# Output projection to up projection: weight sums of the first two units moved ahead, and the last row block put in a manual order

## The chip, the cores and the metric

The kernel runs on one core of a Trainium2 chip. The metric is the device time of one execution in microseconds (us). The kernel before was timed three times: 1768.19, 1768.23 and 1777.83 us, median 1768.23. Engines are named as in the profile: PE is TensorE (matmuls), ACT is ScalarE, DVE is VectorE, POOL is GpSimd, SP is the engine that issues most DMAs; "ur", "wc", "tr" and so on are the program's own names of tiles.

## The reference

One layer of a diffusion backbone over 1024 tokens of width 1024: a modulated norm, neighbourhood attention and retention, a gated merge, an output projection, then a norm and a gated MLP with a short convolution. What matters here is the seam between the output projection and the MLP:

```python
def _merge(o_na, o_ret, gate_na, gate_ret, w_proj_na, w_proj_ret, w_out):
    merged = jax.nn.sigmoid(gate_na) * (o_na @ w_proj_na) + jax.nn.sigmoid(gate_ret) * (o_ret @ w_proj_ret)
    return merged @ w_out

def _conv_ffn(h, w_up, conv_w, conv_b, w_down):
    u = h @ w_up
    ...
    u = sum(up[:, i:i + n] * conv_w[i] for i in range(CONV_W)) + conv_b
    a, val = jnp.split(u, 2, axis=-1)
    return (jax.nn.silu(a) * val) @ w_down

        x = x + g1 * _merge(o_na, o_ret, xga, xgb, w_proj_na[l], w_proj_ret[l], w_out[l])
        hx2 = _modulate(_rmsnorm(x, norm2_g[l]), sh2, sc2)
        x = x + g2 * _conv_ffn(hx2, w_up[l], conv_w[l], conv_b[l], w_down[l])
```

## The kernel before

Every fp32 operand is split into a high and a low part: ACT casts the high part (L86, `split`), DVE subtracts it from the source and leaves the low part (L87), and a product is three matmuls, high by high, high by low, low by high (`mm3` L121 to L123; `open3` L1374). A weight tile of 128x512 comes by an SP DMA into a "raw" or "ur" tile, is split into a "wc" tile (a ring of six), and is then the stationary operand.

**Output projection** (`out_proj`, L1630). Eight blocks of 128 token rows. A block is two column halves ("om") of 24 matmuls each; DVE multiplies a half with the gate (L1642) and adds x (L1643), ACT squares the row and sums it (L1646), DVE scales the sum (L1647), POOL raises it to the power -1/2 (L1648), DVE scales the row (L1649).

**Norm of a block** (`norm_out`, L1652), called one block behind the projection. PE transposes the scaled row, eight 128x128 pieces in two banks (L1664, "tp2", two buffers); for each piece ACT makes the modulated high part "h2h", DVE the modulated value v (L1675) and the low part "h2l" (L1676). From block 4 on DVE makes four combinations of the first and the second token half (L1682 and its neighbours), which go to DRAM (d_t). Block 7, the last, uses banks of the up projection in place of "tp2", and its combinations are split directly.

**Up projection.** Weight columns are worked in units; a unit is a 2x2 block product with seven products in place of eight (`Seven`, class `Up`). The weights of the seven are A11, A12, A22 and four sums S1 to S4 that POOL makes (`load`, L1388 to L1391, 128x512 each); the moving operands are rows of h2 (B11, B21, B22) and the combinations T1 to T4, read back from d_t as "tr" tiles for blocks 4 to 6 and split. Products in PSUM are combined by DVE and ACT (`add` L1403, `close`, `c11` L1838) and the unit ends in `conv` (L1760 and on: one ACT and two DVE instructions for each of two branches, silu, product).

The first two units (`EARLY = 2`) start ahead of the last block's norm: `early_first` makes each unit's A11 product and keeps a copy; `units[0].load()` and `units[1].load()` fetch four weight tiles each and make the sums on POOL; then come block 7's norm, the A12 products, the reading and splitting of twelve "tr" tiles, `open` (the S4 product with B22) and `close` (S1 with T1, S2 with T2, S3 with T3, A22 with T4).

The order of instructions on each engine is made by a scheduler that works from the program's order, a cost model and the dependencies; a block under `tc.manual_schedule()` keeps the order in which it is written. Each engine works its own queue in order and waits on semaphores.

Of the kernel before, what the change touches and what calls it, by code (L numbers as in the profile page):

```python
# [8 lines left out]
F32 = mybir.dt.float32  # L9
# [31 lines left out]
def tile_hybrid_layer(ctx, tc: tile.TileContext, io, dbg=None):  # L41
# [1519 lines left out]
    def gtile(half, dt, name):  # L1561
        return gpool[half].tile([P, 512], dt, tag="g", bufs=2 * KB + 1, name=name)
# [67 lines left out]
    def out_proj(tb):  # L1630
        half, ts = tb // 4, slice((tb % 4) * P, (tb % 4 + 1) * P)
        x1 = op.tile([P, D], F32, tag="x1", bufs=2, name="x1")
        xr = op.tile([P, D], F32, tag="xn", bufs=2, name="xn")
        sync.dma_start(x1, io["x"][tb * P : (tb + 1) * P])
        for dh in range(2):
            cs = slice(dh * 512, dh * 512 + 512)
            m = po.tile([P, 512], F32, tag="o", bufs=2, name="om")
            for kb in range(KB):
                wc = wo[kb, dh]
                h_, l_ = mg[kb, half]  # L1640
                mm3(m, h_[:, ts], l_[:, ts], wc[:, 0], wc[:, 1], kb == 0, kb == KB - 1)
# [7 lines left out]
        vec.tensor_scalar(xr, x1, ss[:, 1:2], None, ALU.mult)  # L1649
        return xr  # L1650

    def norm_out(tb, xr, banks=None):  # L1652
        half, ts = tb // 4, slice((tb % 4) * P, (tb % 4 + 1) * P)
        if tb == 4:
            h2[1] = [None] * KH + [(gtile(0, F32R, "h2h"), gtile(0, F32R, "h2l")) for _ in range(KH)]
        vr = op.tile([P, KB, P], F32, tag="v", bufs=2, name="v")
        if half:
            vo = [gtile(0, F32, "vo").rearrange("p (k t) -> p k t", k=KH) for _ in range(2)]
            for i in range(2):
                sync.dma_start(vo[i], d_h[tb - 4, :, i * KH : i * KH + KH])  # L1660
        for kg in (1, 0):
            tp = banks[kg].rearrange("p (k t) -> p k t", k=4) if banks else po.tile([P, 4, P], F32, tag="t", bufs=2, name="tp2")
            for k in range(4):
                pe.transpose(tp[:, k], xr[:, (kg * 4 + k) * P : (kg * 4 + k + 1) * P], ident)  # L1664
            for k in range(4):
                kb = kg * 4 + k
                t = h2[half][kb]
                a, sh = a2[:, kb : kb + 1], col[:, 24 + kb : 25 + kb]
                v = vr[:, kb]
                if t is None:  # L1670
                    act.activation(v, tp[:, k], AF.Identity, bias=sh, scale=a)
                    continue
# [8 lines left out]
        (b11, b21), b12, b22 = vo, vr[:, :KH], vr[:, KH:]
        vec.tensor_tensor(b11, b12, b11, ALU.subtract)  # L1682
        vec.tensor_tensor(b12, b22, b12, ALU.subtract)
        vec.tensor_tensor(b22, b22, b11, ALU.subtract)
        vec.tensor_tensor(b21, b21, b22, ALU.subtract)
        for c, t in enumerate((b11, b22, b12, b21)):
            if banks:
                split(combs[f"T{c + 1}"][0][:, tb - 4], combs[f"T{c + 1}"][1][:, tb - 4], t)
            else:
                act.dma_start(d_t[c, tb - 4], t)  # L1690

    xr = None
    for tb in range(NTB):
        nx = out_proj(tb)
# [8 lines left out]
    seq = [j + NH * i for j in range(NH) for i in range(2)]  # L1703
    EARLY = 2

    def early_bank(n):
        return u_tile(2 * n), u_tile(2 * n + 1)

    def early_prod(bank, n, i):
        w = wload(io["w_up"][seq[n], 0, i])  # L1710
        for k in range(KH):
            x = h2[0][i * KH + k]
            open3(bank, w[:, 0, k * P : (k + 1) * P], w[:, 1, k * P : (k + 1) * P], x[:, 0], x[:, 1], i == 0 and k == 0, i == 1 and k == KH - 1)

    def early_first(n):
        early.append(early_bank(n))
        early_prod(early[n][0][:, 0:512], n, 0)
        early_p1.append(gtile(0, F32, "pu"))
        act.copy(early_p1[n], early[n][0][:, 0:512])

    early, early_p1, combs, traw = [], [], {}, {}
    early_first(0)
    po.release()
    pu.append(ps("u_ps1", "left"))
    wop.release()
    gpool[1].release()
    early_first(1)


    rp = sb("raws", "right")  # L1730
    tpl = sb("combs", "right")
    A11, A12, A22, S1, S2, S3, S4 = range(7)
# [52 lines left out]
    class Up(Seven):  # L1785
# [16 lines left out]

        def open(self):
            self.banks()
            self.p1 = early_p1[self.n]
            self.c11()
            self.W = early[self.n][1][:, 512:1024]
            self.prod(self.W, self.s4, "B22", True, True)

        def close(self, n):  # L1810
            if n == 0:
                self.prod(self.Z, self.s1, "T1", True, True)
            elif n == 1:
                self.u2, self.u3 = (self.tmp() for _ in range(2))
                self.prod(self.Y, self.s2, "T2", True, False)
# [307 lines left out]
```

## Time and profile before

| | us |
|---|---|
| runs | 1768.19, 1768.23, 1777.83 |
| median | 1768.23 |
| profiled execution, its own time | 1775.33 |
| its span | 1773.2 |
| TensorE busy in it | 1724.2 (97%) |

Times of the trace are microseconds from the start of the span. The output projection's block 6 runs at about 1085 to 1098, block 7 at 1098 to 1110, and the first two units of the up projection from there to about 1175. In rows of the timeline the bracket holds the idle time of the engine before the instruction and what ended it. The granted clock is a share of TensorE's full 2.4 GHz.

### The profile page before, as it was taken

The page shows a single profiled execution, that of the slowest core. Times are in us where ns is not written, and L with a number is a line of the kernel's source. Part 1 is how long each engine was busy: PE and PEld are TensorE (multiplying, and loading weights), DVE is VectorE, ACT ScalarE, POOL GpSimd, SP SyncE. Part 2 cuts the span into 40 slices and gives each one's busy share as a digit, 9 for nine tenths or more (in the row PEclk, how much of TensorE's full clock was granted, in tenths as well). Part 3 has the DMA queues.
Part 4 walks back from the last instruction along what each step waited for, and adds up shares of the span by engine and source line. Part 5 has one row for each costly group of instructions (what it writes and reads, how often), then busy time and mean ns, then how long its engine had stood idle before and what let it go on. Part 6 is the DMA issues. An engine that isn't in the chain of part 4 may idle for free.

```text
span 1773.2 us, 24636 instructions
## 1 busy us (share of the span) xinstructions
PE 1724.2 (97%) x8333; PEld 1428.0 (81%) x8333; DVE 1312.6 (74%) x2444; ACT 854.8 (48%) x1843; POOL 581.5 (33%) x485
## 2 busy tenths in 40 slices
PE   8799999999999999999999999799999999999997
PEld 3588888888888888788888888677888888788886
DVE  4878888765776766777665556898889989875755
ACT  4666667653443434453444324544444444554444
POOL 2510000002233343555423300355455555211444
PEclk9799999999999999999999999899999999999999
DMA  9133433433221212576658634632322333585754
GB/s 344 43 119 109 135 112 115 141 104 126 73 92 60 81 39 81 172 238 222 219 175 306 217 142 169 212 102 89 112 96 89 110 118 100 164 287 191 245 160 164
DMA packets 139550, 260.55 MB, mean 147 GB/s; under 512 B 15872, under 2 KB 28320, under 8 KB 139424
## 3 DMA queue, kind: packets, MB, share of 16 engines
q1 hardware_dynamic: 118048, 228.57, 39.4%
q10 hardware_dynamic: 21376, 30.42, 4.7%
q8 instruction: 65, 1.06, 0.2%
q14 instruction: 61, 0.50, 0.1%
HBM read 187.87 MB, written 68.44 MB: 145 GB/s over the span
## 4 chain that ended last, share of the span: by engine, by line
PE 44%; issue 5%; DVE 4%; POOL 3%; ACT 1%; DMA 1%; POOLq 0%; ACTq 0%; DVEq 0%; SPq 0%
PE u L1374 29%; PE y L1374 4%; PE pr L111 2%; PE pr L110 2%; PE pr L112 2%; PE om L123 2%; PE om L122 2%; PE om L121 2%; DVE wc L87 1%; POOL x L1937 1%; PE pn L112 1%; PE pn L111 1%; PE pn L110 1%; POOL pd L1974 0%; DVE at L1761 0%
## 5 line engine op out<-in xcount | busy, mean ns | idle before, releaser
L1374 PE MATMUL u<-T,wc 128*128 128x512 f32 x1056 | 251.1, 393 | 3.7 <-DVE T L87 2.2
L1374 PEld LDWEIGHTS u<-T,wc 128*128 128x128 f32 x1056 | 198.5, 189 | 50.5 <-ACT pu L1413 3.0
L1374 PE MATMUL y<-wc,ahl 128*128 128x512 f32 x924 | 210.6, 390 | 2.1 <-DVE wc L87 1.8
L1374 PEld LDWEIGHTS y<-wc,ahl 128*128 128x128 f32 x924 | 173.3, 188 | 39.1 <-DVE wc L87 2.5
L87 DVE TENSOR_TENSOR wc<-ur,wc 128x512 fp32r<-128x512 f32 x139 | 124.9, 900 | 63.7 <-ACT wc L86 63.7
L86 ACT CAST wc<-ur 128x512 fp32r<-128x512 f32 x139 | 86.3, 622 | 123.2 <-PE y L1374 72.8
L1374 PE MATMUL u<-h2a,wc 128*128 128x512 f32 x528 | 127.7, 397 | 3.5 <-DVE pu L1422 2.8
L111 PE MATMUL mm<-low,wc 128*128 128x512 f32 (+1 forms) x328 | 123.9, 378 | 0.0
L1374 PEld LDWEIGHTS u<-h2a,wc 128*128 128x128 f32 x528 | 100.4, 191 | 25.7 <-issue 2.4
L110 PE MATMUL mm<-hx,wc 128*128 128x512 f32 x264 | 107.5, 407 | 0.3 <-DVE vc L221 0.3
L112 PE MATMUL mm<-hx,wc 128*128 128x512 f32 x264 | 105.0, 398 | 0.0
L86 ACT CAST wc<-s 128x512 fp32r<-128x512 f32 x88 | 54.2, 622 | 98.5 <-PE u L1374 95.4
L1513 POOL TENSOR_TENSOR col<-col,bcol 128x32 f32<-128x32 f32 x1 | 0.3, 251 | 282.4 <-DVE aw L538 282.4
L123 PE MATMUL mm<-wc,low 128*128 128x512 f32 (+1 forms) x240 | 91.3, 380 | 0.0
L1374 PE MATMUL u<-hxT,wc 128*128 128x512 f32 x384 | 89.8, 389 | 0.1
L87 DVE TENSOR_TENSOR wc<-s,wc 128x512 fp32r<-128x512 f32 x88 | 88.1, 1001 | 0.3
L1374 PEld LDWEIGHTS u<-hxT,wc 128*128 128x128 f32 x384 | 72.0, 188 | 15.4 <-issue 0.5
L87 DVE TENSOR_TENSOR wc<-raw,wc 128x512 fp32r<-128x512 f32 x88 | 65.9, 757 | 22.4 <-ACT wc L86 22.1
L121 PE MATMUL mm<-wc,hx 128*128 128x512 f32 x192 | 75.2, 392 | 0.6 <-ACT r L1105 0.6
L122 PE MATMUL mm<-wc,hx 128*128 128x512 f32 x192 | 75.3, 392 | 0.0
L87 DVE TENSOR_TENSOR wc<-wr,wc 128x512 fp32r<-128x512 f32 x56 | 55.9, 1001 | 22.4 <-ACT wc L86 20.2
L1388 POOL TENSOR_TENSOR s<-ur 128x512 f32<-128x512 f32 x22 | 34.6, 1574 | 108.7 <-DVE wc L87 79.8
(389 smaller groups left out, 4643.7 us busy)
## 6 DMA issues: line engine op xcount, KB each, us to landing
ur<-in_w_up SPq DMA_DIRECT2D x88, 256.0 KB, 2.8
ur<-d_a SPq DMA_DIRECT2D x77, 256.0 KB, 3.2
aw<-in_w_ada SPq DMA_DIRECT2D x32, 512.0 KB, 3.3
pj<-in_w_down SPq DMA_DIRECT2D x44, 256.0 KB, 4.7
d_w<-pj SPq DMA_DIRECT2D x44, 256.0 KB, 2.0
d_a<-sa SPq DMA_DIRECT2D x44, 256.0 KB, 2.0
ur<-d_w SPq DMA_DIRECT2D x44, 256.0 KB, 3.5
d_a<-at SPq DMA_DIRECT2D x33, 256.0 KB, 2.6
```

The source lines that it names most:

```text
L86: act.copy(hi, src)
L87: (lo_eng or vec).tensor_tensor(lo, src, hi.bitcast(F32), ALU.subtract)
L110: pe.matmul(out, wh, xh, start=k == 0, stop=False)
L111: pe.matmul(out, wh, xl, start=False, stop=False)
L112: pe.matmul(out, wl, xh, start=False, stop=k == n - 1)
L121: pe.matmul(out, ah, bh, start=first, stop=False)
L122: pe.matmul(out, ah, bl, start=False, stop=False)
L123: pe.matmul(out, al, bh, start=False, stop=last)
L1374: pe.matmul(out, a, b, start=first and n == 0, stop=last and n == 2, skip_group_check=True)
L1388: pin(pool.tensor_tensor(self.s1, self.a21, self.a22, ALU.add))
L1513: pool.tensor_tensor(col[:, 16:48], col[:, 16:48], bcol[:, 16:48], ALU.add)
L1937: pool.tensor_tensor(z, z, fg[:, gs(dh)], ALU.mult)
```

## The change

1. *Sums ahead of time.* A generator `up_sums` makes S1 to S4 of the first two units on POOL during the output projection, two sums after each of the blocks 1 to 6 until all eight are made. Its loads (four tiles for each unit) use the three "raw" buffers; each sum is stored by an SP DMA to a new DRAM array d_u, and is loaded again ("ur") where its product needs it. The loads of A11 and A12 as moving parts of the early products stay, so the weights of these units pass over the DMA queues more than once: eight stores and about ten loads of 256 KB more, some 4.7 MB.
2. *Functions taken apart.* `out_proj` and `norm_out` become `out_begin`, `out_mm`, `out_add`, `norm_square`, `norm_scale`, `norm_begin`, `norm_turn`, `norm_rows`, `norm_comb`, `store_comb`. With `va=True` `norm_rows` makes v on ACT in place of DVE. The row's square is issued before its store to d_x1. The combinations are made in the order T1, T3, T2, T4.
3. *A manual order* for block 7, block 6's norm, the early products (A11, A12, S4 with B22, S1 with T1 of both units), block 7's norm and the splits of T1, T2 and of block 7's T3 and T4. Block 6's transposes stand between the halves of block 7.
4. *Fewer steps behind it.* `open` only copies; `close` has three steps; the splits of the "tr" tiles of T3 and T4 come after the S2 products of both units.

```diff
-    def out_proj(tb):
+    def up_sums():
+        for n in range(EARLY):
+            t0, t1, t2 = up_raw(n, 1, 0), up_raw(n, 1, 1), up_raw(n, 0, 0)
+            for c, o, x, y, f in ((0, t1, t0, t1, ALU.add), (2, t0, t2, t0, ALU.subtract), (1, t2, t1, t2, ALU.subtract), (3, None, None, t2, ALU.subtract)):
+                if o is None:
+                    o = x = up_raw(n, 0, 1)
+                late(pool.tensor_tensor(o, x, y, f))
+                sync.dma_start(d_u[n, c], o)
+                yield
...
-            vec.tensor_tensor(xr[:, cs], m, gate1[:, cs], ALU.mult)
-            vec.tensor_tensor(x1[:, cs], xr[:, cs], x1[:, cs], ALU.add)
-        act.dma_start(d_x1[tb * P : (tb + 1) * P], x1)
-        ss = op.tile([P, 2], F32, tag="ss", bufs=2, name="ss")
-        act.activation(xr, x1, AF.Square, accum_out=ss[:, 0:1])
...
+        act.activation(t["n"], t["x"], AF.Square, accum_out=ss[:, 0:1])
+        act.dma_start(d_x1[tb * P : (tb + 1) * P], t["x"])
...
+            if t is None or va:
+                act.activation(v, tp[:, k], AF.Identity, bias=sh, scale=a)
+            else:
                 vec.tensor_scalar(v, tp[:, k], a, sh, ALU.mult, ALU.add)
...
+        norm_square(tb)
+        norm_scale(tb)
         if tb:
-            norm_out(tb - 1, xr)
-        xr = nx
+            norm_out(tb - 1)
+            next(usums, None)
+            next(usums, None)
...
+    with tc.manual_schedule():
+        out_begin(LAST)
+        ra = [up_raw(n, 0, 0) for n in range(EARLY)]
+        norm_begin(LAST - 1)
+        norm_begin(LAST)
+        out_mm(LAST, 0)
+        wu[0, "a11"], wu[1, "a11"] = w_split(ra[0]), w_split(ra[1])
+        norm_turn(LAST - 1, 1)
+        norm_turn(LAST - 1, 0)
+        out_add(LAST, 0)
+        out_mm(LAST, 1)
+        tr = {(0, b): comb_raw(0, b) for b in range(2)}
+        norm_rows(LAST - 1, 1, True)
+        norm_rows(LAST - 1, 0)
...
+        mm_seven(early[0][0][:, 0:512], wu[0, "a11"], h2_rows(0, 0), True, False)
+        out_add(LAST, 1)
+        norm_square(LAST)
...
+        norm_scale(LAST)
+        wu[0, "a12"] = w_split(ra[0])
+        norm_turn(LAST, 1, early[0][1][:, 0:512])
+        norm_turn(LAST, 0, early[1][1][:, 0:512])
...
+        wu[0, "s4"] = w_split(us[0, 3])
+        norm_rows(LAST, 1, True)
+        norm_rows(LAST, 0)
...
+        t0 = norm_comb(LAST, 0)
+        wu[0, "s1"] = w_split(us[0, 0])
+        for b in range(3):
+            comb_split(0, b, tr[0, b])
+        comb_split(0, 3, t0)
+        mm_seven(early[0][1][:, 0:512], wu[0, "s1"], comb_rows("T1"), True, True)
...
+        comb_split(2, 3, t2)
+        comb_split(3, 3, t3)
...
-    units[0].load()
...
-    norm_out(NTB - 1, xr, (early[1][1][:, 0:512], early[0][1][:, 0:512]))
-    for n in range(EARLY):
-        early_prod(early[n][0][:, 0:512], n, 1)
-    for c in (0, 1, 2, 3):
...
-    units[1].load()
     units[0].open()
     units[1].open()
-    for i, n in ((0, 0), (1, 0), (0, 1), (1, 1), (0, 2), (0, 3), (1, 2), (2, -1), (1, 3)):
+    units[0].close(0)
+    units[1].close(0)
+    for c in (2, 3):
+        for b in range(3):
+            comb_split(c, b, comb_raw(c, b))
+    for i, n in ((0, 1), (0, 2), (1, 1), (2, -1), (1, 2)):
```

On PE before, the end of the last projection block and what follows it; "tp_" are the transposes of block 6, "u<-ident,xn" those of block 7, "u<-h2a,wc" the early products with A11 and A12:

```order
L123 MATMUL om<-wx,ml 128x512
L1664 MATMUL tp_11831<-ident,xn 128x128 x4
L1664 MATMUL tp_11848<-ident,xn 128x128 x4
L1374 MATMUL u<-h2a,wc 128x512 x12
L1664 MATMUL u<-ident,xn 128x128 x4
L1374 MATMUL u<-h2a,wc 128x512 x17
L1664 MATMUL u<-ident,xn 128x128 x4
L1374 MATMUL u<-h2a,wc 128x512 x19
L1374 MATMUL u<-h2h,wc 128x512
```

On PE after, the middle of the last projection block (between its two halves) and then its end:

```order
L123 MATMUL om<-wo,ml 128x512
L1693 MATMUL tp_11846<-ident,xn 128x128 x4
L1693 MATMUL tp_11851<-ident,xn 128x128 x4
L121 MATMUL om<-wc,mh 128x512
...
L123 MATMUL om<-wx,ml 128x512
L1374 MATMUL u<-h2a,wc 128x512 x24
L1693 MATMUL u<-ident,xn 128x128 x8
L1374 MATMUL u<-h2a,wc 128x512 x24
L1374 MATMUL u<-h2h,wc 128x512
```

Block 6's eight transposes moved half a block earlier; block 7's moved from behind one A11 product and into the middle of the A12 products to a place behind both A11 products.

On DVE before, around the first half of block 7; "v_" and "h2l_" belong to block 5:

```order
L1642 TENSOR_TENSOR xn_11764<-om_11766,gate1_10277 128x512
L1676 TENSOR_TENSOR h2l_11619<-v_11724,h2h_11618 128x128
L1675 TENSOR_SCALAR v_11724<-tp2_11729,a2_8902,col_83 128x128
L1643 TENSOR_TENSOR x1_11763<-xn_11764,x1_11763 128x512
L1676 TENSOR_TENSOR h2l_11621<-v_11724,h2h_11620 128x128
```

And on DVE after, at the same place:

```order
L1663 TENSOR_TENSOR xn_11799<-om_11815,gate1_10277 128x512
L1710 TENSOR_TENSOR h2l_11652<-v_11757,h2h_11651 128x128
L1664 TENSOR_TENSOR x1_11798<-xn_11799,x1_11798 128x512
L1708 TENSOR_SCALAR v_11757<-tp2_11762,a2_8902,col_83 128x128
L1710 TENSOR_TENSOR h2l_11648<-v_11805,h2h_11647 128x128
```

The last reading of block 5's bank (the v) moved behind the add of block 7's first half.

On ACT after, behind the manual block; "uu" are the copies of `c11` of units 0 and 1, wc_12302 and wc_12360 are weights of unit 2, wc_12320 is an A22, "ta" is the convolution of unit 0, T30 the splits of T3 from "tr" tiles, T40_11958<-vo_11812 the last split of the manual block:

```order
L86 CAST wc_12302<-ur_12283 128x512
L86 CAST T40_11958<-vo_11812 128x512
L1958 COPY uu_12142<-u_11905 128x512
L1958 COPY uu_12145<-u_11968 128x512
L86 CAST wc_12320<-ur_12318 128x512
L86 CAST wc_12360<-s_12288 128x512
L1884 ACTIVATE ta_12250<-uu_12142,cb_12140,cw_12138 128x1024
L86 CAST T30_11956<-tr_12188 128x512
L86 CAST T30_11956<-tr_12192 128x512
L86 CAST T30_11956<-tr_12196 128x512
```

Before, the copies stood among the splits of T2; now they stand behind the last split of the manual block and behind the cast of a weight of unit 2, and the T3 splits from "tr" tiles stand behind two more weights and the first instruction of a convolution.

## Rows read from the trace of the kernel before

**Rows 1.** The page's share of each engine, and the clock in 40 slices.

```profile
PE 1724.2 (97%) x8333; PEld 1428.0 (81%) x8333; DVE 1312.6 (74%) x2444; ACT 854.8 (48%) x1843; POOL 581.5 (33%) x485
...
PEclk9799999999999999999999999899999999999999
```

**Rows 2.** Timeline of PE, 1118 to 1200, instructions that follow a wait (start, duration).

```profile
1118.84 1.12 PE L1664 MATMUL u<-ident,xn 128*128 128x128 f32 x4 [5.85 <-DVE xn L1649]
...
1127.83 3.03 PE L1374 MATMUL u<-h2a,wc 128*128 128x512 f32 x12 [0.72 <-ACT pu L1719]
...
1138.92 10.04 PE L1374 MATMUL u<-T,wc 128*128 128x512 f32 x36 [2.17 <-DVE T L87]
1149.31 6.85 PE L1374 MATMUL u<-T,wc 128*128 128x512 f32 x27 [0.35 <-DVE wc L87]
...
1156.78 4.59 PE L1374 MATMUL u<-T,wc 128*128 128x512 f32 x19 [0.62 <-DVE pu L1821]
...
1175.14 3.02 PE L1374 MATMUL u<-T,wc 128*128 128x512 f32 x12 [0.40 <-DVE pu L1416]
...
1199.61 4.38 PE L1374 MATMUL u<-h2a,wc 128*128 128x512 f32 x12 [2.04 <-DVE pu L1422]
```

**Rows 3.** Stretches: length; busy PE, PEld, DVE, ACT, POOL; clock; DMA; GB/s.

```profile
1050.00:1060.00 10.00, 10.00 (x50) 8.38 (x49) 7.87 (x23) 4.48 (x10) 0.55 (x1) 1.00 0.58 207
...
1118.80:1127.80 9.00, 8.27 (x32) 6.53 (x32) 9.00 (x15) 2.93 (x6) 5.36 (x4) 0.80 0.44 121
1127.80:1138.90 11.10, 8.92 (x38) 7.06 (x38) 10.17 (x18) 9.68 (x20) 1.69 (x1) 1.00 0.89 297
1138.90:1149.30 10.40, 10.04 (x36) 7.85 (x36) 9.94 (x12) 7.34 (x14) 4.63 (x3) 0.84 0.43 144
...
1199.60:1210.00 10.40, 10.39 (x39) 8.38 (x40) 6.81 (x9) 3.52 (x6) 0.40 (x1) 0.84 0.36 108
```

**Rows 4.** Timeline of POOL and DVE ahead of the 5.85 us wait.

```profile
1112.67 1.27 POOL L1388 TENSOR_TENSOR s<-ur 128x512 f32<-128x512 f32 x1 [11.18 <-DMA ur<-in_w_up]
...
1117.04 1.74 DVE L1649 TENSOR_SCALAR xn<-x,ss 128x1024 f32<-128x1024 f32 x1 [3.86 <-POOL ss L1648]
```

**Rows 5.** Timeline of all engines, blocks 6 and 7 of the output projection.

```profile
1090.57 0.33 SPq L1634 DMA_DIRECT2D x<-in_x  x1
...
1098.23 0.48 PE L121 MATMUL om<-wo,mh 128*128 128x512 f32 x1
...
1099.46 1.06 ACT L1646 ACTIVATE xn<-x 128x1024 f32<-128x1024 f32 x1
...
1101.52 0.75 DVE L1649 TENSOR_SCALAR xn<-x,ss 128x1024 f32<-128x1024 f32 x1 [0.73 <-POOL ss L1648]
...
1103.77 0.39 PE L121 MATMUL om<-wc,mh 128*128 128x512 f32 x1
1103.97 0.69 DVE L1642 TENSOR_TENSOR xn<-om,gate 128x512 f32<-128x512 f32 x1 [0.25 <-PE om L123]
1104.78 0.40 DVE L1675 TENSOR_SCALAR v<-tp,a,col 128x128 f32<-128x128 f32 x1
```

**Rows 6.** Timeline of DVE and POOL in the splits of T, 1137 to 1149.

```profile
1136.98 3.69 DVE L87 TENSOR_TENSOR T<-tr,T 128x512 fp32r<-128x512 f32 x6
...
1144.56 4.09 DVE L87 TENSOR_TENSOR T<-tr,T 128x512 fp32r<-128x512 f32 x3
1144.69 1.72 POOL L1390 TENSOR_TENSOR s<-ur 128x512 f32<-128x512 f32 x1 [1.90 <-DMA tr<-d_t]
```

**Rows 7.** Groups by form, 1100 to 1160: busy, mean ns | idle before.

```profile
L1838 ACT COPY uu<-u 128x512 f32<-128x512 f32 x2 | 1.2, 576 | 0.0
...
L1760 ACT ACTIVATE ta<-uu,cb,cw 128x1024 f32<-128x1024 f32 x1 | 1.2, 1243 | 1.4 <-DVE uu L1403 1.4
L1761 DVE SCALAR_TENSOR_TENSOR ta<-uu,cw,ta 128x1023 f32<-128x1023 f32 x1 | 1.3, 1268 | 0.0
```

**Rows 8.** DMA issues, 1085 to 1100: KB each, median us to landing.

```profile
x<-in_x SPq DMA_DIRECT2D x1, 512.0 KB, 4.1
```

More of the change, by code (lines that the diff above doesn't have):

```diff
@@ L1628, in tile_hybrid_layer @@
         wo[kb, 1] = wload(io["w_out"][1, kb], into=t)
[L1630 to L1646 removed]
+    seq = [j + NH * i for j in range(NH) for i in range(2)]
@@ new lines, in tile_hybrid_layer, with up_raw @@
+    EARLY = 2
+    d_u = dram.tile([EARLY, 4, P, 512], F32, name="d_u")
+    def up_raw(n, b, i):
+        return rawload(io["w_up"][seq[n], b, i])
+    def up_sums():
[7 more added lines that the diff above has]
+                yield
@@ new lines, in tile_hybrid_layer, with out_begin, out_mm @@
+    tok = [None] * NTB
+    def out_begin(tb):
+        tok[tb] = t = {"x": op.tile([P, D], F32, tag="x1", bufs=2, name="x1"), "n": op.tile([P, D], F32, tag="xn", bufs=2, name="xn")}
+        sync.dma_start(t["x"], io["x"][tb * P : (tb + 1) * P])
+    def out_mm(tb, dh):
+        half, ts = tb // 4, slice((tb % 4) * P, (tb % 4 + 1) * P)
+        m = tok[tb]["m"] = po.tile([P, 512], F32, tag="o", bufs=2, name="om")
+        for kb in range(KB):
+            wc = wo[kb, dh]
+            h_, l_ = mg[kb, half]
+            mm3(m, h_[:, ts], l_[:, ts], wc[:, 0], wc[:, 1], kb == 0, kb == KB - 1)
@@ L1647, in out_proj, with norm_begin @@
         vec.tensor_scalar(ss[:, 0:1], ss[:, 0:1], 1.0 / D, EPS, ALU.mult, ALU.add)
         pool.tensor_tensor(ss[:, 1:2], ss[:, 0:1], mhalf[:, 0:1], ALU.pow)
[L1649 to L1653, printed above, removed]
+        vec.tensor_scalar(t["n"], t["x"], ss[:, 1:2], None, ALU.mult)
+    def norm_begin(tb):
+        t = tok[tb]
         if tb == 4:
             h2[1] = [None] * KH + [(gtile(0, F32R, "h2h"), gtile(0, F32R, "h2l")) for _ in range(KH)]
-        vr = op.tile([P, KB, P], F32, tag="v", bufs=2, name="v")
-        if half:
-            vo = [gtile(0, F32, "vo").rearrange("p (k t) -> p k t", k=KH) for _ in range(2)]
+        t["v"] = op.tile([P, KB, P], F32, tag="v", bufs=2, name="v")
+        if tb >= 4:
+            t["o"] = [gtile(0, F32, "vo").rearrange("p (k t) -> p k t", k=KH) for _ in range(2)]
@@ L1659, in norm_out @@
             for i in range(2):
[L1660 to L1672, printed above, removed]
+                sync.dma_start(t["o"][i], d_h[tb - 4, :, i * KH : i * KH + KH])
@@ new lines, in norm_turn, with norm_rows @@
+    def norm_turn(tb, kg, bank=None):
+        t = tok[tb]
+        t[kg] = tp = bank.rearrange("p (k t) -> p k t", k=4) if bank is not None else po.tile([P, 4, P], F32, tag="t", bufs=2, name="tp2")
+        for k in range(4):
+            pe.transpose(tp[:, k], t["n"][:, (kg * 4 + k) * P : (kg * 4 + k + 1) * P], ident)
+    def norm_rows(tb, kg, va=False):
+        half, ts = tb // 4, slice((tb % 4) * P, (tb % 4 + 1) * P)
+        for k in range(4):
+            kb = kg * 4 + k
+            t, tp = h2[half][kb], tok[tb][kg]
+            a, sh = a2[:, kb : kb + 1], col[:, 24 + kb : 25 + kb]
+            v = tok[tb]["v"][:, kb]
+            if t is not None:
@@ L1681, in norm_out @@
[L1681 to L1690, printed above, removed]
@@ L1692, in tile_hybrid_layer, with norm_comb, store_comb, norm_out @@
-    xr = None
-    for tb in range(NTB):
-        nx = out_proj(tb)
+    def norm_comb(tb, c):
+        (b11, b21), v = tok[tb]["o"], tok[tb]["v"]
+        b12, b22 = v[:, :KH], v[:, KH:]
+        o, x, y = ((b11, b12, b11), (b22, b22, b11), (b12, b22, b12), (b21, b21, b22))[c]
+        vec.tensor_tensor(o, x, y, ALU.subtract)
+        return o
+    def store_comb(tb, c, t):
+        act.dma_start(d_t[c, tb - 4], t)
+    ORDER = (0, 2, 1, 3)
+    def norm_out(tb):
+        norm_begin(tb)
+        for kg in (1, 0):
+            norm_turn(tb, kg)
+            norm_rows(tb, kg)
+        if tb < 4:
+            act.dma_start(d_h[tb], tok[tb]["v"])
+            return
+        for c in ORDER:
+            store_comb(tb, c, norm_comb(tb, c))
@@ L1704, in tile_hybrid_layer @@
-    EARLY = 2
     def early_bank(n):
         return u_tile(2 * n), u_tile(2 * n + 1)
[L1709 to L1732, printed above, removed]
+    def w_split(raw):
+        w = wtile()
+        split(w[:, 0], w[:, 1], raw)
+        return w
+    def mm_seven(bank, w, xs_, first, last):
+        for k, (xh, xl) in enumerate(xs_):
+            open3(bank, w[:, 0, k * P : (k + 1) * P], w[:, 1, k * P : (k + 1) * P], xh, xl, first and k == 0, last and k == KH - 1)
@@ new lines, in h2_rows, with comb_rows, comb_raw, comb_split @@
+    def h2_rows(k0, half):
+        return [(t[:, 0], t[:, 1]) if half == 0 else t for t in h2[half][k0 : k0 + KH]]
+    def comb_rows(c):
+        return [(combs[c][0][:, :, k], combs[c][1][:, :, k]) for k in range(KH)]
+    def comb_raw(c, b):
+        t = gtile(0, F32, "tr")
+        sync.dma_start(t, d_t[c, b])
+        return t
+    def comb_split(c, b, t):
+        split(combs[f"T{c + 1}"][0][:, b], combs[f"T{c + 1}"][1][:, b], t if len(t.shape) == 3 else t.rearrange("p (k t) -> p k t", k=KH))
@@ L1740, in tile_hybrid_layer @@
+    op.release()
+    tap = sb("conv", "right")
+    cw = tap.tile([P, 2 * NF, 3], F32, name="cw")
+    sync.dma_start(cw, io["conv_w"])
+    cb = tap.tile([P, 2 * NF], F32, name="cb")
+    sync.dma_start(cb, io["conv_b"])
+    A11, A12, A22, S1, S2, S3, S4 = range(7)
     class Stream:
```

87 lines of the change are left out of this document (62 added, 25 removed).

## The prediction

> **What bounds the kernel now.** First the page's shares and the clock by slices: PE is busy for 1724.2 of 1773.2 us and its clock is nearly everywhere full [rows 1]. So a change can win only where PE waits, or where its clock falls. Then PE's timeline through the seam: seven waits, 5.85 + 0.72 + 2.17 + 0.35 + 0.62 + 0.40 + 2.04 = 12.15 us [rows 2]. Then the stretches behind the long ones: the granted clock is 0.80, 0.84 and 0.84 there, while in mid-projection, and in the 11.1 us that begin with the wait of 0.72, it is 1.00 [rows 3]. A stretch of 9.0 us at a mean of 0.80 loses 9.0 x 0.20 = 1.8 us, one of 10.4 us at 0.84 loses 1.7, twice: 5.2 in all. The mean lies between the engine's two levels, 2.4 and 1.2 GHz. So the clock falls behind waits of 2.04 us and more, and not behind that of 0.72.
>
> So the change can return at most 12.15 + 5.2 = 17.4 us here, from a kernel of 1768. One per cent is 17.7 us, and 1% is about what a measurement of this kernel can tell from no change. The question is how much of 17.4 comes back, and which waits the new order makes.
>
> Behind the longest wait the chain is plain [rows 4]: the pow of block 7 stands on POOL behind three of the weight sums (1.27 us each, the first at 1112.67), and then the scaling of the row takes 1.74 us on DVE beside the fourth sum. The same instruction took 0.75 us for block 6 [rows 5], with no sum on POOL.
>
> **The change part by part.** The units: 24 projection matmuls go from 1098.23 to 1103.77, so 5.54 us for a half block, and 12 matmuls of a product take 2.77 us [rows 5]. A DVE split is 3.69 / 6 = 0.6 us where POOL is quiet [rows 6]; a cast or copy on ACT 0.58, the first of the convolution 1.24, DVE's next 1.27 [rows 7].
>
> *Sums made earlier.* Eight sums of 1.27 us go to POOL in the projection, two in a block of some 12 us. POOL has 0.55 us of work in 10 us there [rows 3], and a pow that is late by two sums (2.5 us) has nearly a block of slack, since a block's transposes come one block later. The 18 additional transfers of 256 KB meet queues at a DMA share of 0.58 [rows 3]; SP's x loads wait behind the stores of sums by a few us, and are needed over 10 us later. I cost all this at nothing. Without that cover it is the price of a late pow, below 2.5 us a block.
>
> *A. Block 6's transposes between the halves of block 7.* PE gets there at about 1104.3. The second four write the bank that block 5's last v still reads. On DVE this v started at 1104.78 before, directly behind the gate product (1103.97, 0.69 us) [rows 5]; now it stands behind the add too, with two weight splits ahead on DVE. It ends at about 1106.2 plus a semaphore's travel: a wait of 2.2 us. It is new. Low end 1.5 (splits finished early); high end 4.5, if ACT, which has the casts of two early weights ahead of block 5's rows, waits for those loads. I take 2.2, since ACT was at block 6's Square at 1099.46 [rows 5], 5 us ahead of PE's arrival. The clock falls behind a wait of 2 us: 1.7 more.
>
> *B. Block 7's transposes.* The last half ends at about 1114.0. Now two A11 products, 5.5 us, follow in place of one: PE comes at 1119.6. The chain beside them: gate product and add 1.4, Square 1.1 + 0.2, scaling of the sum 0.15, pow 0.55 (POOL's one instruction in [rows 3]'s first stretch) with no sum ahead of it, row 0.75, travel: done at 1118.5. Wait 0 (to 1). This removes 5.85 and 1.8 of clock.
>
> *C. A12 products.* Their weights are loaded and split in time: 0, against 0.72 before; high end 2.3, if the raw tiles come late.
>
> *D. T1 products.* DVE has seven instructions of 0.6 us for block 7's rows and T1 behind ACT's nine; PE has the rest of the A12 and the two S4 products (4 x 2.77 = 11.1 us) as cover. The sums of unit 2 on POOL may fall beside them. I take 1.2 (0 to 1.9), in place of 2.17 and its clock of 1.7.
>
> *E. T2 products.* New: PE's first T2 matmul waits for ACT's copy of unit 0's finished quarter, since that shares a tile with the bank it writes. The copy now stands behind the last split of the manual block. Before it DVE has eleven instructions, 11 x 0.6 = 6.6 us, and two of them may fall beside two POOL sums of unit 2. In the trace three splits beside sums took 4.09 us, not 1.8: 2.3 more [rows 6]. Then cast 0.58, copy 0.58, travel 0.15. Against it stand the two T1 products, 5.54. Without collision 6.6 + 1.3 - 5.54 = 2.4, with it 4.7. Low end 1.75 (DVE runs ahead), high end 5.0. I take 4.6: the trace's own splits fell beside POOL's in just this place. Clock 1.7.
>
> The Trainium skill, page "SBUF — State Buffer", section "Who interferes with whom", says that a DVE instruction with two SBUF inputs and a GpSimd instruction that reads SBUF exclude each other: the later one blocks until the first is done. The trace agrees (4.09 us for three splits, beside a sum that took 1.72 us and not 1.27). By that rule E is 4.7, by two engines that share nothing it is 2.4. The rule also speaks against the sums in the projection, but there POOL's two sums would cost DVE 2.5 us of a block in which it is idle for a fifth.
>
> *F. T3 products.* New: the splits of the "tr" tiles of T3 stand on ACT behind the weight cast of unit 2 (0.6, it waits for the end of the last T2 product because of the ring of six) and the convolution's first instruction (1.24), then come three casts; on DVE 1.27 behind that, an add of 0.6, and three splits of 0.6. From the end of the T2 products: 0.6 + 1.24 + 1.27 + 0.6 + 1.8 less overlap = 5.1 (4.5 to 5.5). Clock 1.7. Before, all T splits were done ahead and this wait was 0.40 to 0.62.
>
> *G. Later waits.* 0.40 and 2.04 before, with 1.7 of clock. The late copies and adds of units 0 and 1 are now fewer behind E and F: 0.4 (0 to 2.44 and the clock's 1.7).
>
> *Sum.* Waits 2.2 + 0 + 0 + 1.2 + 4.6 + 5.1 + 0.4 = 13.5; clock 3 x 1.7 = 5.1; 18.6 in all. Before 17.4. So +1.2 us on the profiled execution's 1775.33, that is 1776.5. That execution is 7.1 us above the median of the runs, 1768.23; the difference is carried over: 1769.5.
>
> Low ends: 1.5 + 0 + 0 + 0 + 1.75 + 4.5 + 0 = 7.75, and two or three clock falls, 3.4 to 5.1: 11.2 to 12.9, which is 5 to 6 us under before. High ends: 4.5 + 1 + 2.3 + 1.9 + 5.0 + 5.5 + 2.44 = 22.6, five falls 8.5: 31, which is 14 over before.
>
> **The rivals.**
> *R1, faster.* DVE keeps up: the T4 split of block 7 runs ahead of PE, POOL's sums of unit 2 come at another moment, and the T3 splits overlap with the convolution. For it: DVE's stretch at 1118.8 to 1127.8 was full (9.00 of 9.00) [rows 3] partly by splits and scaling beside POOL, and eight sums are gone from there. Against it: the places of the copy and of the T3 casts in ACT's queue are fixed. Low ends: 1768.2 - 5.7 = 1762.5.
>
> *R2, slower: the early weights hold ACT.* The casts of the two A11 weights now stand on ACT ahead of block 5's rows and of block 6's Square. Their loads stand on SP behind the x load (issued at 1090.57 before [rows 5]) and "vo" loads; x took 4.1 us to land [rows 8]. From a landing at about 1098.9 on each us holds block 5's rows, so A, by one us: A goes to 4.5, C to 2.3, and there is one clock fall more: 2.3 + 2.3 + 1.7 = 6.3 over the forecast, 1775.8. For it: five transfers queue there. Against it: 1090.57 plus even twice 4.1 is 1098.8, and the new load issue needn't be later than the old.
>
> *R3, it doesn't do what it says.* The sums don't get done during the projection, because the three raw buffers turn too slowly: a sum waits for the store of the one before (some 4 us), so eight sums could reach into block 7, and the pow of block 7 stays behind them. Then B keeps a good part of 5.85 + 1.8, and the time is 1769.5 + 5 = 1774.5. Against it: six blocks of 12 us for eight sums.
>
> **How the numbers follow.** Forecast (two or three new waits eat what the removed ones give): 0.53. R1: 0.27. R2: 0.16. R3: 0.04. The predicted time is the forecast's, 1769.5; its own range is 1766 to 1773. The range 1761 to 1779 takes in R1's and R2's prices and nearly both sums of ends (-6 and +14, less the last part of the latter, since it needs all terms high). Faster by over 1% (below 1750.5) would need more than the 17.4 us that there are: 0.02, for a saving that I don't see. Slower by over 1% (above 1786) is over the sum of all high ends: 0.05. Within 1%: 0.93.
>
> **What would show it right or wrong.** In the changed kernel's PE timeline: no wait of 5.85 us ahead of block 7's transposes, and POOL without sums there (B); a wait of about 2 us ahead of the second four of block 6's transposes, ended by DVE's v or its reader (A); one of 2.4 to 4.7 ahead of the first T2 matmul, ended by ACT's copy (E); one of about 5 ahead of the first T3 matmul, ended by a split of T3 on DVE (F); a clock near 0.84 behind each. If A, E and F are each below 1 us, R1 was right and the gain could reach 12 us or more; if ACT's cast of the first A11 weight waits for its DMA beyond 1099, R2. A kernel below 1761 or above 1779 contradicts the whole sum.

## The result and the profile after

In twenty runs each the kernel before has a median of 1774.21 us and the changed one 1778.84 us; the ratio is 1.0026, 95% interval [1.0016, 1.0037], that is 4.6 us slower and within 1%. (The median of 1768.23 on which the prediction's absolute number stands came from three runs.) The profiled execution took 1779.59 us, its span is 1777.3.

The page of the changed kernel (busy share of each engine; clock in 40 slices), against [rows 1]:

```profile
PE 1721.8 (97%) x8333; PEld 1426.0 (80%) x8333; DVE 1313.6 (74%) x2436; ACT 855.7 (48%) x1851; POOL 583.4 (33%) x485
...
PEclk9899999999999999999999999999999999999999
```

TensorE's timeline of the changed kernel, the instructions behind a wait, against [rows 2]:

```profile
1102.87 0.66 PE L1693 MATMUL tp<-ident,xn 128*128 128x128 f32 x4 [1.57 <-DVE v L1708]
...
1117.38 6.05 PE L1374 MATMUL u<-h2a,wc 128*128 128x512 f32 x24 [2.04 <-ACT wc L86]
1130.16 5.51 PE L1374 MATMUL u<-T,wc 128*128 128x512 f32 x23 [1.07 <-DVE T L87]
1140.11 7.16 PE L1374 MATMUL u<-T,wc 128*128 128x512 f32 x24 [4.44 <-ACT uu L1958]
1150.75 1.22 PE L1374 MATMUL u<-T,wc 128*128 128x512 f32 x2 [3.48 <-ACT T L86]
1154.11 10.83 PE L1374 MATMUL u<-T,wc 128*128 128x512 f32 x34 [2.14 <-DVE T L87]
1178.84 3.04 PE L1374 MATMUL u<-T,wc 128*128 128x512 f32 x12 [0.75 <-DVE pu L1416]
1202.38 2.98 PE L1374 MATMUL u<-h2a,wc 128*128 128x512 f32 x12 [0.63 <-DVE pu L1422]
1205.52 8.48 PE L1374 MATMUL u<-T,wc 128*128 128x512 f32 x36 [0.16 <-ACT pu L1413]
```

The wait of 5.85 us is gone. In its place stand a wait between block 6's two groups of transposes (1.57), one ahead of the A12 products (2.04), one ahead of T1 (1.07), one ahead of T2 (4.44), two ahead of and in T3 (3.48 and 2.14), and 1.54 later: 16.28 us, against 12.15 before. The stretches from the first wait on, in the columns of [rows 3]:

```profile
1102.80:1109.80 7.00, 6.93 (x33) 5.79 (x34) 4.32 (x12) 3.13 (x9) 0.00 (x0) 1.00 0.78 258
1109.80:1117.40 7.60, 5.56 (x30) 4.49 (x28) 3.46 (x7) 2.33 (x5) 0.55 (x1) 1.00 1.04 401
1117.40:1130.10 12.70, 11.69 (x49) 9.02 (x49) 9.56 (x15) 11.45 (x26) 3.26 (x2) 1.00 0.60 219
1130.10:1140.10 10.00, 5.51 (x23) 4.24 (x23) 10.00 (x15) 4.88 (x10) 3.29 (x2) 0.98 0.29 88
1140.10:1150.70 10.60, 7.16 (x24) 5.48 (x24) 7.80 (x12) 4.38 (x8) 4.38 (x4) 0.82 0.64 200
1150.70:1161.10 10.40, 8.21 (x20) 6.03 (x21) 8.21 (x12) 4.51 (x6) 1.60 (x1) 0.54 0.00 0
```

The mean clock is 1.00 behind the waits of 1.57 and 2.04 us and 0.98 behind that of 1.07; behind T2's wait it is 0.82 and behind T3's 0.54. Its price is PE's busy time there times what is missing: 5.51 x 0.02 + 7.16 x 0.18 + 8.21 x 0.46 = 5.2 us. Reckoned in the same way, before had 8.27 x 0.20 + 10.04 x 0.16 + 10.39 x 0.16 = 4.9 [rows 3]; the prediction had 5.2 there, since it took the whole length of the stretches. Waits and clock together are 21.5 against 17.1: 4.4 us more.

The traces agree with that by another way. I call the *seam* the time from the transposes of block 5 (at 1097.44 before, 1094.37 after) to one matmul far behind it, in the last up unit (1538.11 before, 1539.84 after): 440.67 and 445.47 us, 4.8 longer, which is the 4.4 of waits and clock within what these rows resolve. Ahead of the seam the two executions differ by 3.1 us and behind it by 2.4, in opposite directions. The 3.1 us arise ahead of the output projection: from the projection's first matmul (1016.81 before, 1013.73 after) to block 5's transposes both take 80.6 us, although all eight early sums are made in this time in the changed kernel. Below, the seam of a profiled execution stands beside the ratio of the timed runs.

### The profile page after: what moved, and what is told of

It is laid out like the page before. It is cut to its first block, busy times and chain, and to the rows that moved or that the text cites. A ratio compares the mean times of both kernels' runs of the same rounds, so it can differ in the third digit from the quotient of the medians.

```text
span 1777.3 us, 24675 instructions
## 1 busy us (share of the span) xinstructions
PE 1721.8 (97%) x8333; PEld 1426.0 (80%) x8333; DVE 1313.6 (74%) x2436; ACT 855.7 (48%) x1851; POOL 583.4 (33%) x485
## 4 chain that ended last, share of the span: by engine, by line
PE 42%; issue 6%; DVE 4%; POOL 3%; DMA 1%; ACT 1%; SPq 0%; ACTq 0%; POOLq 0%; DVEq 0%
PE u L1374 27%; PE y L1374 4%; PE pr L112 2%; PE pr L111 2%; PE pr L110 2%; PE om L122 1%; PE om L121 1%; PE om L123 1%; DVE wc L87 1%; POOL x L2043 1%; PE pn L112 1%; PE pn L110 1%; PE pn L111 1%; DVE at L1885 1%; DVE ta L1885 0%
## 5 line engine op out<-in xcount | busy, mean ns | idle before, releaser
L87 DVE TENSOR_TENSOR wc<-ur,wc 128x512 fp32r<-128x512 f32 x147 | 133.6, 912 | 64.3 <-ACT wc L86 64.3
L86 ACT CAST wc<-ur 128x512 fp32r<-128x512 f32 x147 | 90.9, 625 | 125.6 <-PE y L1374 72.1
L86 ACT CAST wc<-s 128x512 fp32r<-128x512 f32 x80 | 49.8, 622 | 97.7 <-PE u L1374 93.4
L87 DVE TENSOR_TENSOR wc<-s,wc 128x512 fp32r<-128x512 f32 x80 | 83.2, 1041 | 0.4
```

## The experiments

**e1: another bank.** The first two units' S4 product goes to the tile that ACT copies, T2 to T4 to the other.

```diff
-        mm_seven(early[0][1][:, 512:1024], wu[0, "s4"], h2_rows(KH, 1), True, True)
+        mm_seven(early[0][0][:, 512:1024], wu[0, "s4"], h2_rows(KH, 1), True, True)
...
-            self.X, self.Y, self.Z = t[:, 0:512], t[:, 512:1024], z[:, 0:512]
+            self.X, self.Y, self.Z = t[:, 0:512], (z if self.n < EARLY else t)[:, 512:1024], z[:, 0:512]
```

> The changed kernel, but S4's product goes to the first tile's second bank and T2 to T4 to the second tile's, for the first two units: T2's products no longer share a tile with the quarter that ACT copies. Theory 1 (the copy, by its place in ACT's queue, is what PE waits for): the wait of 4.44 us ahead of the T2 products falls to about 2.7, where the splits of T2 end, and since the scheduler now has unit 2's A11 product ahead of the T3 products, 2.8 us of the T3 waits (3.48 + 2.14) are covered; the seam gets 4 to 6 us shorter, ratio to before 0.999 to 1.001 instead of 1.0026. Rival (DVE's work of the stage is the bound, whichever instruction PE waits at): the T3 splits end when they did, the wait only moves, less than 2 us won, ratio 1.0015 to 1.0026.

Measured 0.9998 [0.999, 1.0007], seam 440.47, 5.0 shorter than after. TensorE's timeline:

```profile
1137.46 0.49 PE L1374 MATMUL u<-T,wc 128*128 128x512 f32 x1 [1.30 <-ACT T L86]
1138.86 5.51 PE L1374 MATMUL u<-T,wc 128*128 128x512 f32 x23 [0.91 <-DVE T L87]
1145.14 3.01 PE L1374 MATMUL u<-h2a,wc 128*128 128x512 f32 x12 [0.77 <-ACT wc L86]
1150.41 0.85 PE L1374 MATMUL u<-T,wc 128*128 128x512 f32 x2 [2.27 <-ACT T L86]
1152.30 18.70 PE L1374 MATMUL u<-T,wc 128*128 128x512 f32 x70 [1.04 <-DVE T L87]
```

T2 now waits 2.21 us for its own splits (1.30 and 0.91), not 4.44 for a copy. Unit 2's product (h2a), which the scheduler now puts ahead of T3, covers part of T3's waits: 3.31 us are left of 5.62. The copy's place was a cost, as theory 1 had it; the 5.0 us are this and the cover together.

**e2: block 6's stores by SP.**

```diff
     def store_comb(tb, c, t):
-        act.dma_start(d_t[c, tb - 4], t)
+        (sync if tb == LAST - 1 else act).dma_start(d_t[c, tb - 4], t)
```

> The changed kernel, but block 6's four combinations are stored by SP's queue and not by ACT's. Theory 1 (the issues of these stores, 2.86 us for two and 0.97 for one while the DMA share is 1.04, hold ACT ahead of the copy and the cast of the first A12 weight): the wait of 2.04 us ahead of the A12 products falls below 0.3 us, later waits stay, ratio to before about 1.0015. Rival (the A12 weights themselves land late, since the sums' way by DRAM fills the queues): ACT is free but its cast waits for the DMA, the wait stays at 1.5 to 2 us, ratio 1.0026.

Measured 0.999 [0.9982, 0.9999], seam 440.18. First the changed kernel's timeline of ACT ahead of the A12 products, then TensorE's of e2:

```profile
1112.25 2.86 ACTq L1720 DMA_DIRECT2D d_t<-v  x2
...
1115.21 0.97 ACTq L1720 DMA_DIRECT2D d_t<-vo  x1
1116.22 0.58 ACT L1787 COPY pu<-u 128x512 f32<-128x512 f32 x1 [3.87 <-PE u L1693]
1116.70 0.62 ACT L86 CAST wc<-raw 128x512 fp32r<-128x512 f32 x1
```

```profile
1103.79 1.12 PE L1693 MATMUL tp<-ident,xn 128*128 128x128 f32 x4 [2.33 <-DVE v L1708]
1135.90 5.74 PE L1374 MATMUL u<-T,wc 128*128 128x512 f32 x24 [1.75 <-ACT uu L1958]
1146.49 1.22 PE L1374 MATMUL u<-T,wc 128*128 128x512 f32 x2 [4.86 <-ACT T L86]
1150.62 10.21 PE L1374 MATMUL u<-T,wc 128*128 128x512 f32 x34 [2.91 <-DVE T L87]
```

Three issues of stores (1.13, 1.57 and 0.97 us) took 3.8 us of ACT, in a stretch with a mean DMA share of 1.04; the nine stores of combinations ahead of them, from 1088.4 on, took 0.33 to 0.95 us. Why these three were long is not shown: a high DMA share alone does not do it, since at a share of 0.97 (1091.9 to 1093.0) two of them took 0.35 and 0.33. ACT's copy and cast stood behind the three. With the stores on SP the A12 wait is gone, so the weights were not late, against the rival. Since block 7's rows then begin earlier on ACT, T1's wait is gone too and T2's is 1.75. I had expected 2 us and the seam gave 5.3: a late start of ACT here is paid again ahead of T1 and T2. T3's wait grew to 7.8.

**e3: T3's splits first.**

```diff
+    for b in range(3):
+        comb_split(2, b, comb_raw(2, b))
     units[0].open()
     units[1].open()
     units[0].close(0)
     units[1].close(0)
-    for c in (2, 3):
-        for b in range(3):
-            comb_split(c, b, comb_raw(c, b))
+    for b in range(3):
+        comb_split(3, b, comb_raw(3, b))
```

> The changed kernel, but the loads and splits of T3's blocks 4 to 6 are written ahead of the first two units' open and T2 products, as all were before. Theory 1 (T3's splits are late only by their place behind a weight of unit 2 and a convolution): the waits of 3.48 and 2.14 us ahead of and in the T3 products fall to below 1 us in all, the wait ahead of T2 grows from 4.44 by 1 to 2.5 us (two or three splits of 0.6 more stand ahead of the copy), and the clock does not fall a second time: 3 to 5 us won, ratio 0.9995 to 1.001. Rival (the tiles' loads are late, whatever the order): ACT waits for them ahead of T2's splits, the T2 wait grows by 3 us or more, ratio 1.002 to 1.004.

Measured 1.0015 [1.0003, 1.0026], seam 444.15: 1.3 us shorter than after.

```profile
1137.99 14.01 PE L1374 MATMUL u<-T,wc 128*128 128x512 f32 x48 [4.22 <-ACT uu L1958]
1154.12 4.57 PE L1374 MATMUL u<-T,wc 128*128 128x512 f32 x12 [2.13 <-DVE pu L1941]
```

T3 (the second half of the 48) waits for nothing, as theory 1 had it, and T2's wait did not grow. But less was won than expected: T4's splits and the convolution came together on DVE, and PE waited 2.13 us there. And the clock, which was to fall only once, was 0.84, 0.72 and 0.83 over some 10 us each behind waits of 2.42 (A12), 4.22 and 2.13 us.

**e4: the sums alone.** In the kernel before, the generator `up_sums` and for units 0 and 1 the following `load`:

```diff
+        def load(self, pin=lambda ins: ins):
+            if self.n >= EARLY:
+                return super().load(pin)
+            self.loaded = True
+            self.s4, self.s1, self.s2, self.s3 = (ur_load(d_u[self.n, c]) for c in (3, 0, 1, 2))
+            self.a22 = ur_load(self.src[1, 1])
```

> The kernel before with part 1 of the change alone: S1 to S4 of the first two units are made in the projection and come back from DRAM, all order is the scheduler's. Theory 1 (the earlier sums are worth what they take from POOL, and their way by DRAM is hidden): block 7's pow has no sums ahead of it, the wait of 5.85 us falls to 2.5 to 3.5 and the scaling to 0.75 us, T1's splits run without collisions; 4 to 6 us won, ratio to before 0.9965 to 0.998. Rival (the added transfers are late or hold queues): the S products wait for their loads, 3 us or more lost elsewhere, ratio 0.999 to 1.003.

Measured 0.995 [0.9938, 0.9962] in five runs, seam 433.18: 7.5 us shorter than before, more than expected.

```profile
1114.13 0.66 PE L1681 MATMUL u<-ident,xn 128*128 128x128 f32 x4 [1.56 <-DVE xn L1666]
1131.58 0.73 PE L1374 MATMUL u<-T,wc 128*128 128x512 f32 x2 [2.51 <-ACT T L86]
1134.63 16.72 PE L1374 MATMUL u<-T,wc 128*128 128x512 f32 x63 [2.31 <-DVE T L87]
1151.97 4.57 PE L1374 MATMUL u<-T,wc 128*128 128x512 f32 x19 [0.62 <-DVE pu L1845]
1192.68 3.00 PE L1374 MATMUL u<-h2a,wc 128*128 128x512 f32 x12 [0.57 <-DVE pu L1422]
```

The 5.85 us are 1.56, and all waits together 7.57. So the first part of the change is a gain by itself, and the way by DRAM is hidden. This kernel is the fastest of the study.

**e5: the changed program in the scheduler's order.**

```diff
-    with tc.manual_schedule():
+    if True:
```

> The changed kernel with its program as it is, but the block under the manual schedule is left to the scheduler. Theory 2 (formed on the first four runs: the early sums alone win 0.5%, so it is the order that costs 0.75%; and what costs is that the written order fixes the places of ACT's and DVE's instructions): the stores and the copies move to better places, the waits of 2.04, 4.44 and 5.62 us shrink to half, ratio to before 0.995 to 0.999. Rival (what costs is the program's own sequence, block 6's transposes between the halves, fewer steps ahead and T3's splits behind T2's products, which the scheduler follows): the same waits at the same places, ratio 1.001 to 1.003.

Measured 0.9991 [0.9982, 1.0], seam 439.02. T2's wait was 3.75, T3's 4.01 and 2.42, that ahead of A12 0.49; those of block 6's transposes and of T1 were gone. So the fixed places cost about 0.35% of time (1.0026 to 0.9991), at the start of the stage above all; but T2's and T3's waits come with the program's own sequence, as the rival had it. The truth lay between the two.

**e6: the order alone.** No d_u; the two units' eight sums on POOL inside the manual block, behind `norm_scale(LAST)`.

```diff
-        us = {(n, c): ur_load(d_u[n, c]) for c in (3, 0, 1) for n in range(EARLY)}
...
         norm_scale(LAST)
+        sums(0)
...
+        sums(1)
```

> The change without its first part: nothing goes by way of DRAM, POOL makes the first two units' sums inside the manual order, behind the pow of block 7. Theory 2 (the two parts add up: the sums by DRAM win 0.5%, the order costs 0.75%): S4's products and T1's wait for POOL's sums, and DVE's two-input instructions collide with them, ratio to before 1.005 to 1.009. Rival (the manual order keeps POOL free in this stage, so that sums behind the pow fit in, and the way by DRAM with its full queues is what costs): the A12 wait of 2.04 us goes, ratio 0.999 to 1.003.

Measured 1.0029 [1.0019, 1.0039]. Theory 2 falls: the two parts do not add up. The order alone costs 0.3%, and with the early sums inside it as much (0.26%); inside the manual order the sums by way of DRAM win nothing that could be measured. The ratio lies in the rival's range, but the rival's mechanism came only in part: ahead of A12 PE still waited 1.19 us (0.98 and 0.21) in place of 2.04, T2's wait was 2.21, and T3's two were 3.48 and 4.75. The profiled execution (1776.26 us, in runs with a median of 1780.32) does not show all of that loss; its seam is only 0.7 us longer than before's.

**e7: e1 and e2 together.**

> The changed kernel with both earlier edits, the other bank for S4 and T2 to T4 and block 6's combinations stored by SP. If the two remove different waits (the copy ahead of T2, and the late A12 cast), their gains of 5.0 and 5.3 us in the seam add up: ratio to before 0.9955 to 0.9975. If both only shorten the same chain on DVE up to T3's splits, one gives most of it: 0.998 to 1.000.

Measured 0.9983 [0.9974, 0.9993], seam 435.43: 10.0 us shorter than after. In the seam that is nearly the sum of 5.0 and 5.3. By the timed ratios it is not: e1 and e2 win 0.28 and 0.36%, the two together 0.43% (7.6 us), which lies in the second range, where both shorten the same chain. Whether the gains add up stays open. PE waits 3.38 us for DVE ahead of unit 2's product now, and 2.27 for T3's splits.

**e8: e4 with block 7's vo loads issued earlier.**

```diff
+    vo_last = vo_load(NTB - 1)
     early_first(0)
```

> The kernel before with the early sums alone (as e4), and the two loads of block 7's first half (vo, from d_h) issued ahead of the units' weights. In e4 DVE's first combination of block 7 waited 3.05 us for them, and PE then 2.51 and 2.31 us for T1's splits. If that load is what ends last, 2 to 4 us more are won and the clock does not fall: ratio to before 0.992 to 0.994. If the T1 splits' own tiles or ACT are late as well, less than 1 us: 0.9945 to 0.9955.

Measured 0.996 [0.9948, 0.9973], no better than e4 and in neither range. The waits for T1's splits went, and PE waited 2.83 us for ACT's copy ahead of its first T product.

**e9, e11: e4 and e8 with e1's exchange of banks.**

```diff
-            self.W = early[self.n][1][:, 512:1024]
+            self.W = early[self.n][0][:, 512:1024]
```

> The kernel before with the early sums alone (as e4), and S4's product and T2 to T4's of the first two units in exchanged banks, so that T2 shares no tile with the quarter that ACT copies. If a copy's place in ACT's queue holds PE in the scheduler's order too (e8 showed PE waiting 2.83 us for it ahead of its first T product), 1 to 3 us more than e4: ratio to before 0.993 to 0.9945. If T1's splits end last in this order (e4 waited 2.51 and 2.31 us for them), the exchange wins nothing: 0.9945 to 0.996.

> e8 (early sums alone, block 7's vo loads issued early) with the exchanged banks of e9. PE's wait of 2.83 us for ACT's copy in e8 should go: ratio to before 0.993 to 0.995. If DVE's splits are next, it stays at 0.9955 to 0.9965.

Measured 1.0003 [0.9992, 1.0015] and 0.9994 [0.9981, 1.0006]: by the timed runs both lose what e4 and e8 had won, outside both ranges. TensorE's timeline of e9:

```profile
1128.68 1.22 PE L1374 MATMUL u<-T,wc 128*128 128x512 f32 x2 [7.15 <-ACT T L86]
1130.72 0.79 PE L1374 MATMUL u<-h2h,wc 128*128 128x512 f32 x1 [0.82 <-ACT uu L1862]
```

In this program S4's product (h2h) is written behind the copy, so in the copy's tile it had to wait for it. The scheduler put the T product ahead, and that waited 7.15 us for its splits. In e11 the same two waits were 4.91 and 2.45. A miss of mine: e1's edit is no gain in another sequence.

**e10: the pow ahead of the sums, and nothing else.** In the kernel before, POOL's first sum waits for DVE's scaling of block 7's row.

```diff
+    def behind_scale(ins):
+        tc.add_manual_dep(ins.ins, scaled[-1].ins.name, mybir.DependencyInfo(mybir.DependencyClass.Sync, mybir.DependencyReason.DATA))
...
-    units[0].load()
+    units[0].load(behind_scale)
```

> The kernel before with one wait added and nothing else: POOL's first weight sum waits for DVE's scaling of block 7's row, so that the pow of block 7 stands ahead of all eight sums; nothing goes by way of DRAM. Theory 3 (both parts of the change remove the same wait, the pow behind the sums, and a few instructions' order is all that this needs): the 5.85 us wait falls to 2 or less, the scaling takes 0.75 us, the sums are done in time for S4 and collide with splits as before; 4 to 7 us won, ratio to before 0.996 to 0.998. Rival (the sums must be out of the stage, since DVE's splits and S4's products then wait for them): the wait comes back ahead of S4 or T1, ratio 0.9985 to 1.001.

Measured 0.9996 [0.9984, 1.0007], seam 445.71 to a mark at which before has 446.11. The timeline of PE, POOL and DVE:

```profile
1111.81 0.66 PE L1669 MATMUL u<-ident,xn 128*128 128x128 f32 x4 [1.12 <-DVE xn L1654]
...
1117.43 1.33 POOL L1388 TENSOR_TENSOR s<-ur 128x512 f32<-128x512 f32 x1
...
1117.54 1.77 DVE L1688 TENSOR_TENSOR v<-v 128x512 f32<-128x512 f32 x1
...
1124.96 5.49 PE L1374 MATMUL u<-h2a,wc 128*128 128x512 f32 x12 [6.53 <-ACT pu L1724]
```

The 5.85 us wait became 1.12, but a new one of 6.53 stands ahead of an A12 product. Between 1111.9 and 1123.4 all eight sums ran on POOL, DVE was busy for 11.47 of these 11.5 us, and its combinations beside the sums took 1.43 to 1.77 us, against 0.68 in e4 with POOL idle. So theory 3 fell: the pow's place is not enough. What e4 wins is that the sums leave the stage in which DVE is busy. The Trainium skill, page "SBUF — State Buffer", section "Who interferes with whom", has such pairs exclude each other; the trace agrees (1.77 us for a DVE combination that began 0.11 us after a sum of 1.33).

**e12: e1, e2 and e3 together.**

> The changed kernel with the three edits of e1, e2 and e3 together: the other bank for S4 and T2 to T4, block 6's combinations stored by SP, T3's loads and splits ahead of the first units' open. Theory 4 (the written order's cost is these three places, and mended it is worth as much as the early sums in the scheduler's order, 0.995): the waits ahead of A12 and in T3 go, of that ahead of T2 less than 3 us are left, ratio to before 0.994 to 0.9965. Rival (DVE, which has 10 of 10 us busy from the norm's rows on, is the bound, so that what is won ahead of T3 is lost ahead of T2): ratio 0.9975 to 0.9995, as e7.

Measured 0.9985 [0.9975, 0.9995], as e7. The rival was right:

```profile
1132.54 1.72 POOL L1390 TENSOR_TENSOR s<-ur 128x512 f32<-128x512 f32 x1
1133.05 4.03 DVE L87 TENSOR_TENSOR T<-tr,T 128x512 fp32r<-128x512 f32 x3
...
1137.14 5.51 PE L1374 MATMUL u<-T,wc 128*128 128x512 f32 x23 [3.71 <-DVE T L87]
...
1193.54 4.48 PE L1374 MATMUL u<-h2a,wc 128*128 128x512 f32 x12 [3.70 <-DVE pu L1422]
```

The A12 and T3 waits are gone. T2 waits 3.71 us for three splits that took 4.03 us beside unit 2's sums, and a new wait of 3.70 us for DVE stands later, ahead of a unit's A11 product (0.57 in e4 at the like place).

## Why the prediction was right, and where it was not

The direction held: no change by over 1%, and the new waits eat up what the old one returns. The sum was 1.2 us over before and is 4.8 in the trace, 4.6 by the timed ratio. The wide range, 1761 to 1779, held by 0.16 us, which is luck as much as reckoning; the forecast's own range, 1766 to 1773, did not. Of the distance from 1769.5 to 1778.84 the larger part is the median of before (1774.21 in place of 1768.23). Taken as a difference to before, the forecast's own range is -2.2 to +4.8, and 4.6 is near its upper end. What the sum missed is 2.04 at C and 1.14 at G; the other waits were off by less than 0.7.

- *A*: 2.2 forecast, 1.57 measured, ended by DVE's v as said. The clock did not fall behind it (1.00), so the 1.7 us for it were too much.
- *B*: 0 and 0. POOL has no sum at block 7; its first one there begins at 1124.42.
- *C* is the step that failed: "Their weights are loaded and split in time: 0" measured 2.04. That is below C's high end of 2.3, but not for the reason given there (raw tiles that come late), as e2 shows, and not for R2's: the first A11 cast began at 1094.69, well before 1099. I counted the stores of block 6's combinations nowhere, though they are issues on ACT's own queue; e2 shows them as the cause, and that the wait's price goes on to T1 and T2.
- *D*: 1.2 and 1.07. *E*: 4.6 and 4.44, ended by ACT's copy, behind two DVE instructions of 1.77 us each beside POOL's sums. e1 confirms that PE waited for the copy. The changed kernel's rows:

```profile
1131.24 1.77 DVE L87 TENSOR_TENSOR wc<-ur,wc 128x512 fp32r<-128x512 f32 x1
1132.54 1.62 POOL L1391 TENSOR_TENSOR s<-ur,s 128x512 f32<-128x512 f32 x1
1132.93 1.77 DVE L1716 TENSOR_TENSOR v<-v,vo 128x512 f32<-128x512 f32 x1
...
1139.48 1.06 ACT L1958 COPY uu<-u 128x512 f32<-128x512 f32 x2
```

- *F*: 5.1 and 5.62, ended by T3's cast and then its split. The clock behind E and F was mis-sized: 3.4 forecast, 5.1 measured (1.3 and 3.8), with 0.54 and not 0.84 in the last stretch, which follows waits of 4.44, 3.48 and 2.14 us. The total for the clock, 5.1 forecast and 5.2 measured, came out by errors that cancel (nothing behind A). *G*: 0.4 and 1.54, with no clock fall.
- *The sums at nothing*: right for their price; the projection takes 80.6 us up to block 5's transposes with them and without. What the prediction did not see is that this part alone wins 0.5% (e4), since it takes POOL from beside DVE (e10), and that the order then gives it back. R1 asked for DVE to keep up, and it did not (10.00 of 10.00 us busy ahead of T2); R3 fell (POOL has one pow and no sum at block 7).
- *The clock's rule*, that it falls behind waits of 2.04 us and more, did not hold: behind 2.04 us it stayed at 1.00 here.

Open: why the manual order, mended at three places (e12), stays 0.35% behind the scheduler's order with early sums (e4). The profiled executions show 2.7 of these 6 us, and where they stand: TensorE's waits are 11.49 us in e12 and 7.57 in e4, with two for DVE of 3.7 us each in e12. Which part of the order makes DVE late is not shown: block 6's transposes between the halves, v on ACT and DVE's order of combinations were not undone one by one.

## What to carry to other kernels

Test the parts of a change by themselves: here one part alone wins 0.5%, the other on top of it loses 0.76% (alone 0.29%), and the whole looks like a small loss. In an order written by hand count every instruction on a queue, DMA issues too, and ask which engine waits behind it; a store issued by a compute engine can hold that engine, here by 3.8 us for three stores. Work of POOL that slows DVE can be moved to where DVE has time, even by way of DRAM: in the scheduler's order that won 0.5%, in the manual order nothing.

## What the runs showed that I had not expected

Two DMA issues on ACT's queue took 2.86 us, where the shortest took 0.33 each. TensorE's granted clock had a mean of 0.54 over 10.4 us behind three waits of 4.44, 3.48 and 2.14 us, and stayed at 1.00 behind waits of 1.57 and 2.04 us; before, it had been 0.84 behind one of 2.04. In e12 it stayed at 1.00 for 20.9 us behind a wait of 3.71 us (1137.1 to 1158.0), and in e2 it was 0.82 behind one of 2.33. So in these traces the length of a wait does not tell by itself whether the clock falls.
